# Last sum of the second pooling unit on VectorE, other PSUM pairs for the last gates, pool weights and recurrence results further forward in their queues

## The chip, the cores and the metric

One core of one Trainium2 chip runs the kernel. The metric is the device time of one execution in microseconds (us), as the median of several runs; the profile is a further execution, recorded by the hardware profiler. The engines are TensorE (PE in the profile), its weight load (PEld), VectorE (DVE), ScalarE (ACT), GpSimd (POOL) and SyncE (SP), which issues DMAs only.

## What is computed

One transformer layer in fp32, for 512 positions of 1024 channels. The reference, cut to its main line:

```python
h = rms_norm(x, norm_mix)
u_pool, u_lru, q, k, v, g_logits = split(h @ w_in)        # 1024 columns each, g_logits 3 x 1024
gates  = sigmoid(g_logits + b_gate)                       # one per branch and channel
y_pool = pool_mixer(u_pool, w_pool, pool_scale)           # means over 2, 4, 8, 16 positions, minus u;
                                                          # then a 256 x 256 product per group of channels
y_lru  = rglru_mixer(u_lru, ...)                          # gated linear recurrence along the positions
y_sb   = stick_breaking_attention(rms(q), rms(k), v)      # 8 heads of 128
merged = sum over b of gates[b] * (y[b] @ w_branch[b])
x = x + merged @ w_out
x = x + swiglu_ffn(rms_norm(x, norm_ffn))
```

## The kernel before

**Products.** Each fp32 product is made of three matmuls in a faster format. `split_w` (L135) takes a weight of 128x1024 elements apart: ScalarE writes the rounded part `whi` (L142), VectorE the rest `wlo` (L143). `product` (L354, its matmuls L359) then issues 24 matmuls of 128x256 columns. Raw weights come in by DMA from SP's queue into tiles named raw, qw (gates and q, k, v) or pw (pooling), each with few buffers: a load waits until the buffer's last reader is done.

**Seven products in place of eight.** The large projections go by a scheme of the Strassen kind: a unit of work has seven products, 11, 12, S1, S2, S3, S4 and 22, and some of them use sums of weight blocks. These sums are made in place, either by a DMA from GpSimd's queue that adds to what is in the buffer (`accum_op`), or by a VectorE addition. `add_pool7` (L255 to L269) does this for the two pooling units: `PNEXT` (L242) names for unit 1 the DMAs that accumulate (after the split of 11, S1 and S2), and unit 0 has its S4 sum on VectorE (L259). `PORDER` (L240) is the order of the products of both units.

**The order of the work around the change.** After q, k and v come the two pooling units (names u and ps_u), then four units of gates of which the last two (cc = 0 and 1, names g and ps_g) matter here. `weights` takes the next split weight from a list in fixed order (`emit_next`), up to three ahead of the product. All instructions are put into order by a scheduler that goes by the order of the code, by priorities and by which buffers are free; each engine then works through its own queue in that order, and an instruction that waits holds up all that stand behind it. Between the products `tick` and `pool_mean` (L944) issue the small operations that belong to other parts: `pool_mean` makes the moving means of the pooling branch on VectorE, and `MEAN` (L967) says behind which products.

**PSUM.** Eight banks. Through the projections they are four pairs (pool `pb`); a product unit holds one pair for X and one for Y. Two halves of a unit are read out by ScalarE early (L977, L1006), the rest is added by VectorE at the end (L982, and L938 in `gate_done` for the gates). `gate_done` then has ScalarE make the sigmoid (L940) and GpSimd's queue store the gate to memory (tiles gd, L942). After the gates the same banks are cut up anew for attention: `pmm` (3 banks, branch products ps_br), `pz` (2 banks, scores z) and `paux` (3 banks, among them the transposes pq). For the last unit the pair of ps_gy1 is banks 0 and 1 and that of ps_gx1 banks 4 and 5; the first transposes pq00 go to bank 5, the first branch product ps_br_1_0_0 to bank 0. A memset of VectorE on a tile `skip_g` takes one pair out of the rotation for this.

**What follows the gates.** For each head `trans` (L1127, matmuls L1131) transposes q and k (tiles at, loaded on SP, L1124) into pq, ScalarE and VectorE split the result (qkh L1134, qkl L1135), TensorE makes the scores z, ScalarE turns them into K and A (L1164, L1165), VectorE scans them (L1168). In between stand the products of the recurrence branch, ps_br (lines 350 to 352 within `mm3`, three matmuls of 128x512 each): their right-hand sides yHH and yHL are loaded back from memory by GpSimd's queue (L1286), their weights are raw97, raw98 and so on. `load_pool_weights` (L1072) loads the four matrices of the pooling branch (rawp, L1074, on SP) and splits them (wph L1076, wpl L1077). The merge (L450) multiplies a branch product by its gate g, which SP loads (L1101) from where `gate_done` stored it.

Of the kernel before, what the change touches and what calls it, by code (L numbers as in the profile page):

```python
# [8 lines left out]
F32 = mybir.dt.float32  # L9
# [56 lines left out]
def layer_kernel(ctx: ExitStack, tc: tile.TileContext, x, xt, vecs, w_in, w_qkv7, w_gate7, w_pool7, w_pool, w_rg, w_ig,  # L66
# [79 lines left out]
    def add_direct(key, src, a, b):  # L146
        def load(n):
            raw = wp.tile([P, a, b], F32, tag="raw", name="raw" + n)
            raws.append(nc.sync.dma_start(raw, src).ins)
            return raw  # L150

        def make(n):
            return split_w(early.pop(key, None) or load(n), [P, a, b], n)
        loads[key] = load
        specs.append((key, make))
# [86 lines left out]
    PNEXT = {"11": ("11", "21"), "S1": ("21", "11"), "S2": ("21", "12")}  # L242
# [12 lines left out]
    def add_pool7(u, nm):  # L255
        def make(n):
            if u == 0 and nm == "S4":
                r = praw[u, "12"]
                dve.tensor_tensor(r, r, praw[u, "S2"], ALU.add)  # L259
            buf = {"S1": "21", "S2": "21" if u else "S2", "S3": "11", "S4": "21" if u else "12"}.get(nm, nm)  # L260
# [222 lines left out]
    with ExitStack() as first:  # L483
# [452 lines left out]
        def gate_done(cc, j, t, ps):  # L936
            v = two2(t)
            dve.tensor_tensor(v, v, in_order2(ps), ALU.add)  # L938
            for w in range(2):
                act(t[:, w, :], t[:, w, :], AF.Sigmoid, scale=-1.0 if j else 1.0,  # L940
                    bias=vcol("b_gate", 16 + 2 * (2 * cc + w) + j))
            nc.gpsimd.dma_start(gd2[cc, j], t)  # L942
# [24 lines left out]
        MEAN = ((0, "S4"), (0, "22"), (1, "S2"), (1, "12"))  # L967
# [20 lines left out]
        for cc in range(2):  # L988
            tx, ty = (b4([2, S], f"g{n}{cc}", "bw"[cc]) for n in "xy")
            if cc:  # L990

                dve.memset(pb.tile([P, 2, S], F32, tag="mm", name="skip_g")[:, 0, 0:1], 0.0)
            Y = pb.tile([P, 2, S], F32, tag="mm", name=f"ps_gy{cc}")
            X = pb.tile([P, 2, S], F32, tag="mm", name=f"ps_gx{cc}")
# [8 lines left out]
            for nm in ORDER:  # L1003
# [9 lines left out]
                if (cc, nm) == (0, "12"):  # L1013
                    with tc.issue_after(state["acc"]):
                        q_scales()
                if cc == 0 and nm in ("S2", "S1", "S3"):
                    load_early({"S2": ("br", 1, 0, 0), "S1": ("br", 1, 0, 1), "S3": ("br", 1, 1, 0)}[nm])
                if cc and nm not in ("11", "22") and means:
# [25 lines left out]
    with ExitStack() as mix:  # L1044
# [27 lines left out]
        def load_pool_weights(g):  # L1072
            raw = rawp[g]
            nc.sync.dma_start(raw, w_pool[g].rearrange("(k p) c -> p k c", p=P))  # L1074
# [207 lines left out]
        for i in range(2):  # L1282
            yhl = [hp.tile([P, 4, S], F32R, tag=f"{t}{i}", name=f"y{t}{i}") for t in ("HH", "HL")]
            for k2 in range(2):
                for t, d in zip(yhl, yd):
                    nc.gpsimd.dma_start(t[:, 2 * k2:2 * k2 + 2, :], d[i][:, 2 * k2:2 * k2 + 2, :])  # L1286
            ylru += [tuple(t[:, k, :] for t in yhl) for k in range(4)]
        for c in range(4):
# [539 lines left out]
```

## Time and profile before

| | |
|---|---|
| median of 3 runs | 879.77 us (879.38 to 882.63) |
| the profiled execution | 886.13 us |
| its span, first to last instruction | 884.3 us |
| TensorE busy | 98% |
| VectorE, ScalarE, GpSimd busy | 85%, 60%, 11% |
| stretch of the pooling and gate units around the change | 260 to 329 us |
| start of attention and the recurrence branch | 329 to 392 us |

The profile gives busy times, not useful ones: a matmul at half clock is busy for twice as long. PEclk is the granted clock, 1.00 being full speed. In the views of instructions each row has the start, the duration, the engine, the line, the operation with its output and inputs, and in brackets how long the engine had been idle before it and what ended that. In the view of waits a row names who waited for what, with total, count and longest. In the view of stretches each row has the length, then busy time and count by engine, the granted clock, the busy share of the DMA engines, and GB/s. A DMA's row on a queue is the time of its issuing; when it has landed is told by the rows "to landing".

### The profile page before, as it was taken

The page shows a single profiled execution, that of the slowest core. Times are in us where ns is not written, and L with a number is a line of the kernel's source. Part 1 is how long each engine was busy: PE and PEld are TensorE (multiplying, and loading weights), DVE is VectorE, ACT ScalarE, POOL GpSimd, SP SyncE. Part 2 cuts the span into 40 slices and gives each one's busy share as a digit, 9 for nine tenths or more (in the row PEclk, how much of TensorE's full clock was granted, in tenths as well). Part 3 has the DMA queues.
Part 4 walks back from the last instruction along what each step waited for, and adds up shares of the span by engine and source line. Part 5 has one row for each costly group of instructions (what it writes and reads, how often), then busy time and mean ns, then how long its engine had stood idle before and what let it go on. Part 6 is the DMA issues. An engine that isn't in the chain of part 4 may idle for free.

```text
span 884.3 us, 14573 instructions
## 1 busy us (share of the span) xinstructions
PE 865.3 (98%) x5707; PEld 796.4 (90%) x5707; DVE 748.1 (85%) x949; ACT 527.8 (60%) x733; POOL 95.8 (11%) x137
## 2 busy tenths in 40 slices
PE   9999999999998997999999999999999999999998
PEld 6888878888898996888889998889999999999998
DVE  6899898989787795897989696699998988998974
ACT  6555989667853565675754544555555555754642
POOL 1110002233324111000001100000000000121200
PEclk9999999999999997999999999999999999999999
DMA  9685355998798379545645965346543434797913
GB/s 334 168 293 182 96 189 168 269 276 241 221 303 198 67 213 318 169 132 167 195 116 140 196 190 186 98 121 166 147 117 97 119 97 134 228 208 202 191 42 120
DMA packets 114469, 157.26 MB, mean 178 GB/s; under 512 B 8288, under 2 KB 86112, under 8 KB 114400
## 3 DMA queue, kind: packets, MB, share of 16 engines
q1 hardware_dynamic: 100864, 107.30, 38.2%
q0 software_dynamic: 13392, 48.76, 24.1%
q8 instruction: 45, 0.74, 0.3%
q10 hardware_dynamic: 144, 0.26, 0.1%
q14 instruction: 24, 0.20, 0.1%
HBM read 135.85 MB, written 18.87 MB: 175 GB/s over the span
## 4 chain that ended last, share of the span: by engine, by line
PE 84%; DVE 5%; ACT 5%; DMA 4%; issue 1%; SPq 0%; ACTq 0%; DVEq 0%
PE ps_y L359 11%; PE ps_q L875 8%; PE ps_x L359 8%; PE ps_dy L1746 5%; PE ps_dx L1746 4%; PE ps_br L352 3%; PE ps_br L350 3%; PE ps_br L351 3%; PE ps_bY L1370 2%; PE ps_gy L359 2%; PE ps_bX L1370 2%; PE ps_gx L359 2%; PE ps_uy L359 2%; PE ps_gate L778 2%; DVE wlo L143 1%; PE ps_lru L350 1%
## 5 line engine op out<-in xcount | busy, mean ns | idle before, releaser
L142 ACT ACTIVATE whi<-raw 128x1024 fp32r<-128x1024 f32 x58 | 61.2, 1055 | 64.6 <-PE ps_br L351 16.8
L143 DVE TENSOR_TENSOR wlo<-raw,whi 128x1024 fp32r<-128x1024 f32 x58 | 70.7, 1220 | 18.2 <-ACT whi L142 17.7
L143 DVE TENSOR_TENSOR wlo<-qw,whi 128x1024 fp32r<-128x1024 f32 x48 | 58.3, 1218 | 14.7 <-ACT whi L142 14.7
L142 ACT ACTIVATE whi<-qw 128x1024 fp32r<-128x1024 f32 x48 | 50.4, 1053 | 31.7 <-PE ps_q L875 10.4
L1531 ACT ACTIVATE wh_S<-w_S 128x1024 fp32r<-128x1024 f32 x36 | 38.2, 1061 | 28.8 <-PE ps_y L359 20.1
L1652 POOL DMA_DIRECT2D dw<-in_w_down_dram x20 | 17.4, 957 | 308.3 <-DMA dw<-in_w_down_dram 252.7
L1532 DVE TENSOR_TENSOR wl_S<-w_S,wh_S 128x1024 fp32r<-128x1024 f32 x36 | 43.8, 1218 | 3.3 <-ACT wh_S L1531 3.3
L1531 ACT ACTIVATE wh<-w 128x1024 fp32r<-128x1024 f32 x27 | 28.6, 1061 | 27.8 <-PE ps_x L359 9.4
L1532 DVE TENSOR_TENSOR wl<-w,wh 128x1024 fp32r<-128x1024 f32 x27 | 32.9, 1219 | 7.9 <-ACT wh L1531 7.9
L1531 ACT ACTIVATE whdS<-dw 128x1024 fp32r<-128x1024 f32 x20 | 21.2, 1061 | 21.6 <-PE ps_dy L1746 10.6
L1532 DVE TENSOR_TENSOR wldS<-dw,whdS 128x1024 fp32r<-128x1024 f32 x20 | 24.2, 1219 | 6.1 <-ACT whdS L1531 6.1
L351 PE MATMUL ps_br<-yHL,whi 128*128 128x512 f32 x64 | 25.6, 400 | 1.5 <-DMA yHL<-ydl 1.5
L350 PE MATMUL ps_br<-yHH,whi 128*128 128x512 f32 x64 | 25.4, 397 | 1.2 <-DVE gy L938 1.2
L1168 DVE TENSOR_TENSOR_SCAN E<-K,ahead 128x512 f32<-128x512 f32 (+3 forms) x32 | 25.3, 812 | 1.2 <-ACT K L1164 1.2
L352 PE MATMUL ps_br<-yHH,wlo 128*128 128x512 f32 x64 | 25.4, 397 | 0.0
L350 PE MATMUL ps_lru<-HH,whi 128*128 128x512 f32 x64 | 24.6, 384 | 0.0
L350 PE MATMUL ps_br<-yph,whi 128*128 128x512 f32 x64 | 24.5, 383 | 0.0
L143 DVE TENSOR_TENSOR wlo<-pw,whi 128x1024 fp32r<-128x1024 f32 x13 | 15.9, 1222 | 10.0 <-ACT whi L142 10.0
L350 PE MATMUL ps_gate<-HH,whi 128*128 128x512 f32 x64 | 24.4, 381 | 0.0
L351 PE MATMUL ps_lru<-HL,whi 128*128 128x512 f32 x64 | 24.3, 379 | 0.0
L352 PE MATMUL ps_lru<-HH,wlo 128*128 128x512 f32 x64 | 24.3, 379 | 0.0
L351 PE MATMUL ps_gate<-HL,whi 128*128 128x512 f32 x64 | 24.3, 379 | 0.0
(785 smaller groups left out, 3559.5 us busy)
## 6 DMA issues: line engine op xcount, KB each, us to landing
qw<-in_w_qkv_dram SPq DMA_DIRECT2D x24, 512.0 KB, 7.1
raw<-in_w_in_dram SPq DMA_DIRECT2D x23, 512.0 KB, 5.9
dw<-in_w_down_dram POOLq DMA_DIRECT2D x20, 512.0 KB, 7.6
w<-in_w_ffn_gate_dram SPq DMA_DIRECT2D x36, 256.0 KB, 4.0
w<-in_w_ffn_up_dram SPq DMA_DIRECT2D x36, 256.0 KB, 4.6
raw<-in_w_branch_dram SPq DMA_DIRECT2D x13, 512.0 KB, 4.0
qw<-in_w_qkv_dram POOLq DMA_DIRECT2D x12, 512.0 KB, 8.5
qd<-r POOLq DMA_DIRECT2D x12, 512.0 KB, 6.7
```

The costliest lines, as they stand in the source:

```text
L142: act(hi, raw, AF.Copy)
L143: los.append(dve.tensor_tensor(lo, raw, hi.bitcast(F32), ALU.subtract).ins)
L350: nc.tensor.matmul(ps, lh, rh, start=start, stop=False, skip_group_check=skip)
L351: nc.tensor.matmul(ps, lh, rl, start=False, stop=False, skip_group_check=skip)
L352: nc.tensor.matmul(ps, ll, rh, start=False, stop=stop, skip_group_check=skip)
L359: nc.tensor.matmul(o, a_[a][:, w, k, :], il2(b_[b][:, k, :]), start=first and n == k == 0, stop=last and n == 2 and k == 3, skip_group_che ...
L875: nc.tensor.matmul(ps[:, a, :], b_[:, k, ts_], il(a_[:, kk, :]), start=first and n == k == 0, stop=n == 2 and k == 3, skip_group_check=True)
L1168: dve.tensor_tensor_scan(E[:, c0:c0 + n][:, ::-1], K[:, c0 + 1:c0 + n + 1][:, ::-1], ahead[:, S - n:][:, ::-1], 0.0, ALU.mult, ALU.add)
L1370: nc.tensor.matmul(o, ah[x_][:, w, k, :], il2(b[k][y_]), start=first_ and n == k == 0, stop=n == 2 and k == 3, skip_group_check=True)
L1531: act(h, src, AF.Copy)
L1532: dve.tensor_tensor(l, src, h.bitcast(F32), ALU.subtract)
L1746: nc.tensor.matmul(o, a_[a][:, w, k0 + k, :], il2(b_[b][:, k, :]), start=first and i == k == 0, stop=last and i == 2 and k == nk - 1, skip ...
```

## The change

Its parts, in the order of the diff (lines behind L141 stand one to three lower in the changed kernel):

- The DMA raw97 (first of the branch weights that are not loaded early) is issued only behind the last pool weight on SP; the others follow it.
- The S4 sum of pooling unit 1 is made by VectorE, pw112 += pw121, in place of the accumulating DMA; the query scales, whose issue point hung on that DMA, now follow the accumulation behind S1.
- Three of the eight pooled means are issued in the pooling units, behind other products than the four before; one more is issued in gate unit 0, the rest in gate unit 1.
- The memset of `skip_g` is gone, and unit 1 takes its pair X first: ps_gx1 is now banks 0 and 1, ps_gy1 banks 4 and 5. A memset of GpSimd on a buffer of the raw weights (`skip_r`) is added in gate unit 0.
- On GpSimd the stores of the last two gates are put behind the loads of the recurrence results.

```diff
@@ add_direct
-            raws.append(nc.sync.dma_start(raw, src).ins)
+            with tc.issue_after(state["rawp"]) if key == ("br", 1, 1, 1) else nullcontext():
+                raws.append(nc.sync.dma_start(raw, src).ins)
@@ add_pool7
-    PNEXT = {"11": ("11", "21"), "S1": ("21", "11"), "S2": ("21", "12")}
+    PNEXT = {"11": ("11", "21"), "S1": ("21", "11")}
...
-            if u == 0 and nm == "S4":
+            if nm == "S4":
                 r = praw[u, "12"]
-                dve.tensor_tensor(r, r, praw[u, "S2"], ALU.add)
-            buf = {"S1": "21", "S2": "21" if u else "S2", "S3": "11", "S4": "21" if u else "12"}.get(nm, nm)
+                dve.tensor_tensor(r, r, praw[u, "21" if u else "S2"], ALU.add)
+            buf = {"S1": "21", "S2": "21" if u else "S2", "S3": "11", "S4": "12"}.get(nm, nm)
@@ gate_done
-            nc.gpsimd.dma_start(gd2[cc, j], t)
+            state["gd", cc, j] = nc.gpsimd.dma_start(gd2[cc, j], t).ins
@@ pooling units
-        MEAN = ((0, "S4"), (0, "22"), (1, "S2"), (1, "12"))
+        MEAN = ((1, "12"), (1, "S3"), (1, "22"))
@@ last gate units
-            if cc:
-
-                dve.memset(pb.tile([P, 2, S], F32, tag="mm", name="skip_g")[:, 0, 0:1], 0.0)
-            Y = pb.tile([P, 2, S], F32, tag="mm", name=f"ps_gy{cc}")
-            X = pb.tile([P, 2, S], F32, tag="mm", name=f"ps_gx{cc}")
+            YX = {z: pb.tile([P, 2, S], F32, tag="mm", name=f"ps_g{z}{cc}") for z in ("xy" if cc else "yx")}
+            Y, X = YX["y"], YX["x"]
...
+                if (cc, nm) == (0, "11"):
+                    nc.gpsimd.memset(wp.tile([P, 1024], F32, tag="raw", name="skip_r")[:, 0:1], 0.0)
...
-                if cc and nm not in ("11", "22") and means:
+                if (cc or nm == "S2") and nm not in ("11", "22") and means:
                     pool_mean(*means.pop(0))
@@ load_pool_weights
-            nc.sync.dma_start(raw, w_pool[g].rearrange("(k p) c -> p k c", p=P))
+            state["rawp"] = nc.sync.dma_start(raw, w_pool[g].rearrange("(k p) c -> p k c", p=P)).ins
@@ recurrence results
-                    nc.gpsimd.dma_start(t[:, 2 * k2:2 * k2 + 2, :], d[i][:, 2 * k2:2 * k2 + 2, :])
+                    load = nc.gpsimd.dma_start(t[:, 2 * k2:2 * k2 + 2, :], d[i][:, 2 * k2:2 * k2 + 2, :]).ins
             ylru += [tuple(t[:, k, :] for t in yhl) for k in range(4)]
+        for j in range(2):
+            tc.add_manual_dep(state["gd", 1, j], load.name, mybir.DependencyInfo(
+                mybir.DependencyClass.NoSync, mybir.DependencyReason.DATA), reason="order")
```

What the scheduler makes of it stands in the engines' queues. First VectorE, from wlo75 (the split for product S2 of pooling unit 1) over wlo76 (product 12) to wlo77 (S3); pw112 and pw121 are raw weight blocks of unit 1, u00 and u01 the results of unit 0, pw00 a pooled mean. The split for S4, wlo78, stands five rows behind the end of this piece. Before:

```order
L143 TENSOR_TENSOR wlo75_2498<-pw121_2171,whi75_2497 128x1024
L982 TENSOR_TENSOR u00_2272<-u00_2272,ps_ux0_2307 128x1024
L143 TENSOR_TENSOR wlo76_2533<-pw112_2213,whi76_2532 128x1024
L952 COPY pw00_2527<-u00_2272 128x1
L953 TENSOR_TENSOR pw00_2527<-u00_2272 128x511
L958 SCALAR_TENSOR_TENSOR pw00_2527<-pw00_2527,invpos_112 128x1
L982 TENSOR_TENSOR u01_2308<-u01_2308,ps_uy0_2271 128x1024
L143 TENSOR_TENSOR wlo77_2566<-pw111_2169,whi77_2565 128x1024
```

In the changed kernel, with wlo78 at the end:

```order
L143 TENSOR_TENSOR wlo75_2498<-pw121_2171,whi75_2497 128x1024
L983 TENSOR_TENSOR u00_2272<-u00_2272,ps_ux0_2307 128x1024
L143 TENSOR_TENSOR wlo76_2527<-pw112_2213,whi76_2526 128x1024
L260 TENSOR_TENSOR pw112_2213<-pw112_2213,pw121_2171 128x1024
L983 TENSOR_TENSOR u01_2308<-u01_2308,ps_uy0_2271 128x1024
L143 TENSOR_TENSOR wlo77_2556<-pw111_2169,whi77_2555 128x1024
L143 TENSOR_TENSOR wlo78_2586<-pw112_2213,whi78_2585 128x1024
```

The addition to pw112 stands ahead of the second sum u01, and the three operations of a pooled mean between wlo76 and wlo77 have gone further back, behind wlo78.

SP's queue, from the end of the gates' weights (the row after qw4220 in both) to the loads of the first gates for the merge (g100, g101). Before:

```order
L149 DMA raw97_3524<-in_w_branch_dram 128x4x256
L149 DMA raw98_3616<-in_w_branch_dram 128x4x256
L149 DMA raw99_3691<-in_w_branch_dram 128x4x256
L1074 DMA rawp0_3233<-in_w_pool_dram 128x2x256
L1074 DMA rawp1_3234<-in_w_pool_dram 128x2x256
L1074 DMA rawp2_3231<-in_w_pool_dram 128x2x256
L1074 DMA rawp3_3232<-in_w_pool_dram 128x2x256
L1124 DMA at02_3230<-qd20_88 128x4x128
L1124 DMA at10_3364<-qd00_84 128x4x128
L1124 DMA at11_3366<-qd10_86 128x4x128
L1124 DMA at12_3368<-qd20_88 128x4x128
L1101 DMA g100_3442<-gd10_94 128x512
```

In the changed kernel:

```order
L1074 DMA rawp0_3233<-in_w_pool_dram 128x2x256
L1074 DMA rawp1_3234<-in_w_pool_dram 128x2x256
L1074 DMA rawp2_3231<-in_w_pool_dram 128x2x256
L1074 DMA rawp3_3232<-in_w_pool_dram 128x2x256
L150 DMA raw97_3524<-in_w_branch_dram 128x4x256
L1124 DMA at02_3230<-qd20_88 128x4x128
L150 DMA raw98_3616<-in_w_branch_dram 128x4x256
L1124 DMA at10_3364<-qd00_84 128x4x128
L1124 DMA at11_3366<-qd10_86 128x4x128
L1124 DMA at12_3368<-qd20_88 128x4x128
L150 DMA raw99_3691<-in_w_branch_dram 128x4x256
L1101 DMA g100_3442<-gd10_94 128x512
```

The four rawp have moved ahead of raw97, and at02, at10, at11 and at12 stand between and behind the branch weights; raw99 and g100 are now behind at12. The buffer that at11 takes is one of which GpSimd's store gd211 has to be done.

GpSimd's queue, from the last load for the first two recurrence results to the store of the last gate. Before:

```order
L1286 DMA yHL0_3431<-ydl0_104 128x1024
L1286 DMA yHL1_3437<-ydl1_105 128x1024
L1286 DMA yHH1_3436<-ydh1_103 128x1024
L942 DMA gd210_100<-gx1_2959 128x1024
L1286 DMA yHH1_3436<-ydh1_103 128x1024
L942 DMA gd211_101<-gy1_2960 128x1024
L1286 DMA yHL1_3437<-ydl1_105 128x1024
```

In the changed kernel:

```order
L1286 DMA yHL0_3431<-ydl0_104 128x1024
L1286 DMA yHL1_3437<-ydl1_105 128x1024
L1286 DMA yHH1_3436<-ydh1_103 128x1024 x2
L1286 DMA yHL1_3437<-ydl1_105 128x1024
L943 DMA gd210_100<-gx1_2961 128x1024
L943 DMA gd211_101<-gy1_2962 128x1024
```

Both stores, gd210 and gd211, now stand behind all loads.

## The prediction

> **What bounds the kernel now.** I read the page first, then the view of the waits around the changed code, then the busy times of the stretches, and last the order of single instructions at each stall. The page:
>
> ```profile
> span 884.3 us, 14573 instructions
> PE 865.3 (98%) x5707; PEld 796.4 (90%) x5707; DVE 748.1 (85%) x949; ACT 527.8 (60%) x733; POOL 95.8 (11%) x137
> ```
>
> TensorE is busy for 98% of the span, so there are two ways to gain: shorten a wait of TensorE, or the time that it is busy at a lower clock. The view of what TensorE waits for between 250 and 440 us lists the first:
>
> ```profile
> PE ps_uy L359 <- ACT u L977: 2.8, 1, 2.8
> PE z L350 <- ACT A L1165: 2.3, 1, 2.3
> PE ps_br L351 <- DMA yHL<-ydl: 1.5, 1, 1.5
> PE pq L1131 <- issue: 1.5, 1, 1.5
> PE ps_br L350 <- DVE gy L938: 1.2, 1, 1.2
> PE z L351 <- DVE qkl L1135: 0.4, 1, 0.4
> ```
>
> These six rows are 9.7 us, and nearly all of them lie in the code that the change touches. The busy times of seven short stretches show the second kind of loss (columns: length, busy time and count, granted clock, share of the DMA engines, GB/s):
>
> ```profile
> 278.72:281.71 2.99, 0.17 (x3) 1.00 0.65 214
> 281.71:285.10 3.39, 3.39 (x16) 0.51 0.47 134
> 328.99:332.84 3.85, 1.24 (x11) 1.00 0.99 308
> 332.84:336.40 3.56, 3.56 (x9) 0.52 0.92 292
> 342.80:344.43 1.63, 0.15 (x1) 1.00 1.07 372
> 345.40:347.90 2.50, 0.16 (x1) 0.75 1.16 320
> 347.90:353.30 5.40, 5.40 (x14) 0.50 1.16 317
> ```
>
> After three of the four gaps TensorE runs at half clock for 3.4 to 5.4 us. That costs 3.39 x 0.49 = 1.7, 3.56 x 0.48 = 1.7 and 5.40 x 0.50 = 2.7 us, and it counts as busy. Only the gap of 1.63 us is followed by none. So there are two places to account for: stall 1 at 279 us, and stall 2, a chain of waits from 329 to 353 us.
>
> **Stall 1: the sum by VectorE (L259, L268).** ScalarE's rows and GpSimd's:
>
> ```profile
> 272.44 0.85 POOL L268 DMA_DIRECT2D pw<-in_w_pool_dram  x1 [4.03 <-DVE wlo L143]
> 280.11 1.06 ACT L142 ACTIVATE whi<-pw 128x1024 fp32r<-128x1024 f32 x1 [5.59 <-DMA pw<-in_w_pool_dram]
> 281.08 0.58 ACT L977 ACTIVATE u<-ps_uy 128x512 f32<-128x512 f32 x1
> 257.10 1.23 DVE L259 TENSOR_TENSOR pw<-pw,ps 128x1024 f32<-128x1024 f32 x1
> ```
>
> The accumulating DMA of unit 1 is issued at 272.44 and its sum is there at 280.11, when ScalarE's split of it starts. Behind that split in ScalarE's queue stands the eviction of ps_uy at 281.08, for which TensorE waits: it starts S3 at 281.71. What is late is thus not the product that needs the sum (S4, one later), but an eviction queued behind it. The change sums with a VectorE operation of the last row's shape, 1.23 us, placed behind the split wlo76. VectorE has a gap for it: in 260:282 it is busy for 12.84 of 22.00 us.
>
> ```profile
> 260.00:282.00 22.00, 19.18 (x171) 18.99 (x170) 12.84 (x16) 9.59 (x12) 10.23 (x9) 0.99 0.96 248
> 282.00:304.00 22.00, 22.00 (x185) 22.00 (x185) 19.01 (x24) 9.96 (x12) 1.83 (x2) 0.93 0.43 96
> ```
>
> The sum is then there at about 275.5, ScalarE splits it and reads ps_uy out while TensorE runs the product 12 ahead of S3, and S3 starts when TensorE is free, at 278.7. **Gain: 2.8 us of wait and 1.7 us of half clock, 4.5 us.** Lower bound 2.8, if the half clock comes after another short gap instead. What is late next: VectorE's splits of the gate weights. In 282:304 it has 3.0 us left, the new operation takes 1.2, and part of the pooled means is now issued behind these splits; so I expect no new wait here, with a slack of about 1 us. The memset that goes, the memset that GpSimd gains (in a stretch in which it has nothing due) and the later issue point of the query scales I set at nothing: none stands ahead of something that TensorE awaits.
>
> **Stall 2, first part: the other PSUM pairs.** TensorE's and VectorE's rows:
>
> ```profile
> 329.30 1.21 DVE L938 TENSOR_TENSOR gx<-gx,ps_gx 128x1024 f32<-128x1024 f32 x1
> 331.57 1.21 DVE L938 TENSOR_TENSOR gy<-gy,ps_gy 128x1024 f32<-128x1024 f32 x1
> 330.62 1.06 PE L1131 MATMUL pq<-idn,at 128*128 128x128 f32 x8 [1.46 <-issue]
> 332.84 0.69 PE L350 MATMUL ps_br<-yHH,whi 128*128 128x512 f32 x1 [1.15 <-DVE gy L938]
> ```
>
> The eight transposes pq start when VectorE has read ps_gx (329.30 + 1.21 = 330.51), the branch product when it has read ps_gy (332.78): their new PSUM tiles lie in those banks. The change swaps the pairs. Now pq lies where ps_gy was and must wait for the second sum; the branch waits for the first, but stands behind pq in TensorE's queue. So the transposes no longer fill the time between the two sums, and the branch starts 1.06 us later against the end of the gates. **Cost: 1.1 us** (bounds: 0, if VectorE reaches ps_gy sooner, to 1.1, all eight transposes). The half clock behind this gap I leave as it is.
>
> **Stall 2, second part: pool weights ahead of the branch weights (SP), recurrence results ahead of the gate stores (GpSimd).**
>
> ```profile
> 345.55 0.63 ACT L1076 ACTIVATE wph<-rawp 128x512 fp32r<-128x512 f32 x1 [4.70 <-DMA rawp<-in_w_pool_dram]
> 347.17 0.68 ACT L1165 ACTIVATE A<-z,qrs 128x512 f32<-128x512 f32 x1
> 329.41 5.13 SPq L149 DMA_DIRECT2D raw<-in_w_branch_dram  x3
> 334.60 4.36 SPq L1074 DMA_DIRECT2D rawp<-in_w_pool_dram  x4
> 339.00 7.54 SPq L1124 DMA_DIRECT2D at<-qd  x4
> rawp<-in_w_pool_dram SPq DMA_DIRECT2D x4, 256.0 KB, 10.6
> 334.50 0.54 POOL L942 DMA_DIRECT2D gd<-gy  x1 [1.19 <-ACT gy L940]
> 335.03 0.55 POOL L1286 DMA_DIRECT2D yHL<-ydl  x1
> 321.54 1.22 DVE L143 TENSOR_TENSOR wlo<-qw,whi 128x1024 fp32r<-128x1024 f32 x1
> yHL<-ydl POOLq DMA_DIRECT2D x1, 512.0 KB, 9.4
> ```
>
> The third score product z waits until ScalarE has read the first scores (A, 347.17). ScalarE stands for 4.70 us in front of the pool weight's split wph, whose load went out at 334.60, behind three branch weights that had waited in SP's queue for free buffers until 329.41. It takes 10.6 us to land. With the four loads ahead of those three, they go out when their own buffers come free; the last of these is read by VectorE's split of the gates' last but one weight (321.54 + 1.22 before, so about 318 with 4.5 us gained). Landed after 10.6 us, at 329, they are there before ScalarE arrives. **Gain: 2.3 us of wait and 2.7 us of half clock, 5.0 us**; lower bound 2.3. The last load yHL stood behind the store gd of gy (334.50) and landed 335.03 + 9.4 = 344.4, when TensorE's wait for it ends; ahead of the stores it goes out when the gates still run. **Gain: 1.5 us.** Without the pool weights the 1.5 us would only lengthen the wait for A behind it, so the two go together.
>
> **What this adds.** SP's load at11 takes the buffer of gy, which comes free when the store gd of gy has landed; behind it stand at12, a branch weight and the gates g100. The store is issued 4.5 us earlier than 334.50, at 330.0.
>
> ```profile
> gd<-gy POOLq DMA_DIRECT2D x1, 512.0 KB, 8.1
> g<-gd SPq DMA_DIRECT2D x1, 256.0 KB, 5.4
> 354.87 0.68 DVE L450 SCALAR_TENSOR_TENSOR m<-g,ps_br 128x512 f32<-128x512 f32 x1
> ```
>
> Landing after 8.1 us gives 338.1; two loads at 7.54/4 = 1.9 us and one at 5.13/3 = 1.7 us bring g100's issue to 343.6, and 5.4 us later, at 349.0, the gates are there. TensorE needs what the merge m frees (the PSUM tile of ps_br_1_1_1) 47 matmuls behind z0_2. I put z0_2 at about 341.5: 347.90, less 4.5, less the waits of 1.5 and 2.3, plus 1.1, plus 0.9 for the branch products now ahead of it. At 0.215 us apiece 47 matmuls end at 351.6, so there are 2.6 us left. In VectorE's queue the merge has two weight splits more ahead of it; and later VectorE itself is close to the bound:
>
> ```profile
> 370.00:392.00 22.00, 21.20 (x128) 18.11 (x127) 21.58 (x33) 17.33 (x36) 0.00 (x0) 1.00 0.55 162
> 392.00:530.00 138.00, 137.43 (x880) 125.85 (x879) 118.45 (x176) 80.37 (x143) 9.56 (x11) 1.00 0.62 162
> ```
>
> These two meeting points no row prices. The nearest are the waits of 0.4 (for qkl) and 1.5 us (for yHL) above; I take 0.7 for each, **cost 1.4 us**, with bounds of 0.4 and 3.0. Behind 392 us TensorE is busy for 137.43 of 138.00 us, so nothing there can take up a gain made ahead of it.
>
> **Sum.** 4.5 - 1.1 + 5.0 + 1.5 - 1.4 = 8.5 us. The profiled execution took 886.13 us (its span 884.3); it would be 877.6. The median of the runs shown is 879.77, 6.4 us under the profiled one, and I carry the difference over: 879.77 - 8.5 = **871.3 us**. Ends: all waits and half clocks gone, no cost of pq and the small cost, 4.5 + 5.0 + 1.5 - 0.4 = 10.6, and the half clock at 332.84 too, 1.7 and some tenths: 866.8 or a little under. The other way 2.8 - 1.1 + 2.3 + 1.5 - 3.0 = 2.5: 877.3. The smallest difference that a measurement here tells from none is about 0.5%, 4.4 us: faster means under 875.4.
>
> **The clock, weighed.** Gaps of 2.99 and 2.50 us are followed by half clock at 0.51 and 0.50, the one of 1.63 us is not. The Trainium skill, "TensorE: Matmul & The Clock Gate", Part 1: The HAM clock gate, says that TensorE falls to half rate after an idle window of about 3.4 us, that the windows run free of the program, and that some 3.4 us of work bring it back. By that threshold neither gap had to throttle, and the 4.4 us of clock in my gains would be chance; the trace disagrees with it on the gap's length and agrees roughly on the return (3.39 us, but also 5.40).
>
> **Rivals.**
> *Only stall 1 pays.* VectorE, 21.58 of 22.00 us in 370:392, becomes the bound and stall 2's gain is given back there: 4.5 - 0.7 = 3.8, 876.0. For it: that row. Against it: from 329 to 347 VectorE idles for half of the time, waiting for the same loads, and would start earlier too. Chance 0.10.
> *The half clock stays.* It depends on where a window falls, not on a gap's length, and each stretch comes back after some gap that remains (the one at the gates' end does): 8.5 - 1.7 - 2.7 = 4.1, 875.7. For it: the 1.63 us gap without one. Against it: three of three gaps of 2.5 us and more have one. Chance 0.07.
> *VectorE's queue is too full at stall 1.* The sum delays a split of the gates, and TensorE waits there: with 4.5 lost, 4.0 is left, 875.8. Speaks for it: 19.01 of 22.00 us; against it: the 3.0 us left. Chance 0.05.
> *Slower: SP stands behind the store.* at11 holds up g100 and all later loads. From a landing of the store 2.6 us beyond 338.1 on, each us is one of TensorE's. With 9 us of wait and two half clock stretches behind it (1.7 + 2.7), 13.4 us, it outweighs the gain: 884.7. That needs store and load together to take 25 us instead of 13.5; the slowest landing in the rows above is 10.6. Chance 0.07.
> *The change doesn't reach the wait.* z's wait is set by something that came at the same time as rawp, and S3's by another eviction: about 879.8. Against it: the two releasers are named in ScalarE's rows with 5.59 and 4.70 us of idling. Chance 0.03.
>
> **Chances.** The forecast, with all terms within their bounds, has 0.68. Faster by over 0.5%: the forecast and a little of the three rivals at 876, 0.70. Within 0.5%: the rest of these and the last, 0.23. Slower: 0.07. The range from 866.5 to 877.3 leaves out the slower rival, the last one and some tails of the forecast, near 0.2.
>
> **What would show it.** The profile after should have no wait of ps_uy for u, with S3 at full clock; the transposes pq waiting for gy's sum, near 328; wph with no wait for rawp; no wait for yHL; half clock once, not twice, between 329 and 353; and a small wait, if any, of ps_br for the merge. A long row of SP ahead of at11 with a wait of TensorE for m would prove me wrong, as would VectorE busy all through 282:304 with TensorE waiting for wlo.

## The result, and the profile after

The changed kernel takes 876.12 us (median of 8 runs, 874.58 to 878.29); before took 880.25 us (8 runs, 879.38 to 882.94) on the same chip: a ratio of 0.9948, 95% interval 0.9931 to 0.9965. It is 4.1 us faster (3.1 to 6.1 by the interval), where 8.5 were forecast; 876.12 lies inside the forecast's range, near its upper end. A second comparison on another chip, below, gave 875.54 against 881.13 us, 0.9927 (0.9903 to 0.9951). Ratios and intervals throughout come from the comparison with the kernel before on the same chip, and need not be the quotient of the two medians. One execution of fill (3193.81 us) and one of best_no_sum (1107.16 us) stood far outside all others and are left out of their medians below.

The profiled executions lie much further apart than the medians: 874.58 us after, 886.13 us before. The page after:

```profile
span 872.8 us, 14573 instructions
PE 859.7 (98%) x5707; PEld 791.0 (91%) x5707; DVE 748.5 (86%) x949; ACT 528.3 (61%) x733; POOL 96.6 (11%) x137
```

What TensorE waits for between 250 and 440 us, in full:

```profile
PE pq L1131 <- issue: 3.7, 1, 3.7
PE pq L1131 <- DVE wtl L1184: 0.4, 1, 0.4
PE ps_uy L360 <- DVE wlo L143: 0.3, 1, 0.3
PE pps L352 <- DVE p00l L1041: 0.3, 1, 0.3
PE pw L1181 <- DVE qkl L1135: 0.3, 1, 0.3
PE py L351 <- DVE wtl L1184: 0.2, 1, 0.2
```

The waits for u, for A and for yHL are gone. One has grown: pq waits 3.7 us where it waited 1.5. Single instructions, stall 1 first:

```profile
276.07 1.23 DVE L260 TENSOR_TENSOR pw<-pw,pw 128x1024 f32<-128x1024 f32 x1
277.41 1.07 ACT L142 ACTIVATE whi<-pw 128x1024 fp32r<-128x1024 f32 x1 [2.52 <-DVE pw L260]
278.39 0.57 ACT L978 ACTIVATE u<-ps_uy 128x512 f32<-128x512 f32 x1
279.06 0.32 PE L360 MATMUL ps_uy<-hT3h,whi 128*128 128x256 f32 x1
```

The sum takes 1.23 us, ScalarE's split follows it, the eviction follows the split, and S3 starts at 279.06 with no gap (281.71 before). There is little to spare: the eviction ends 0.1 us before S3 starts (278.39 + 0.57 = 278.96), as the sum is there at 277.30, where I had put 275.5. Stall 2:

```profile
325.53 1.22 DVE L939 TENSOR_TENSOR gx<-gx,ps_gx 128x1024 f32<-128x1024 f32 x1
327.80 1.22 DVE L939 TENSOR_TENSOR gy<-gy,ps_gy 128x1024 f32<-128x1024 f32 x1
329.11 1.94 PE L1131 MATMUL pq<-idn,at 128*128 128x128 f32 x8 [3.72 <-issue]
331.68 0.62 ACT L1076 ACTIVATE wph<-rawp 128x512 fp32r<-128x512 f32 x1
300.28 19.11 SPq L1074 DMA_DIRECT2D rawp<-in_w_pool_dram  x4
324.45 0.57 POOL L1286 DMA_DIRECT2D yHL<-ydl  x1
339.14 0.98 SPq L1101 DMA_DIRECT2D g<-gd  x2
```

The transposes start when gy's sum is done (327.80 + 1.22 = 329.02). The pool weights go out between 300 and 320 us and ScalarE's split wph no longer waits. The last yHL goes out at 324.45. The gates for the merge are issued at 339.14, 4.5 us earlier than I had put them (343.6), and no wait for the merge appears.

The clock, in stretches of 3.41 us (length, TensorE's busy time and count, granted clock, DMA share, GB/s):

```profile
325.02:328.44 3.42, 0.37 (x4) 1.00 0.93 244
328.44:331.85 3.41, 2.74 (x11) 0.50 1.06 361
331.85:335.26 3.41, 3.41 (x18) 1.00 1.07 384
```

One half clock stretch is left between 250 and 800 us, behind the grown gap.

**Where the time went, by parts of the program.** All kernels make their weight splits in the same order on VectorE, so the same split marks the same place in each. Two of the marks as VectorE's rows show them, first in the kernel before:

```profile
328.17 1.22 DVE L143 TENSOR_TENSOR wlo<-rawbr,whi 128x1024 fp32r<-128x1024 f32 x1
...
421.76 1.23 DVE L143 TENSOR_TENSOR wlo<-raw,whi 128x1024 fp32r<-128x1024 f32 x1 [0.18 <-ACT whi L142]
```

The same two in the changed kernel:

```profile
324.40 1.22 DVE L143 TENSOR_TENSOR wlo<-rawbr,whi 128x1024 fp32r<-128x1024 f32 x1
...
413.98 1.23 DVE L143 TENSOR_TENSOR wlo<-raw,whi 128x1024 fp32r<-128x1024 f32 x1 [0.19 <-ACT whi L142]
```

From the first to the second it is 93.59 us before and 89.58 after: the attention start gains 4.0. In the same way the pooling and gate units (from the split at 254.10 us before, 253.86 after, to the first mark) go from 74.06 to 70.54, 3.5 less, and a part of the FFN near 800 us (from the split at 771.28 to the one at 821.32 us before) from 50.05 to 46.17, 3.9 less. These three make up 11.4 of the 11.5 us between the spans. Nothing of the change touches the FFN.

### The profile page after: what moved, and what is told of

It reads as the page before. It is cut to its first block, busy times and chain, and to the rows that moved or that the text cites. A ratio compares the mean times of both kernels' runs of the same rounds, so it can differ in the third digit from the quotient of the medians.

```text
span 872.8 us, 14573 instructions
## 1 busy us (share of the span) xinstructions
PE 859.7 (98%) x5707; PEld 791.0 (91%) x5707; DVE 748.5 (86%) x949; ACT 528.3 (61%) x733; POOL 96.6 (11%) x137
## 4 chain that ended last, share of the span: by engine, by line
PE 87%; DVE 5%; ACT 4%; issue 2%; DMA 1%; SPq 0%; DVEq 0%; ACTq 0%
PE ps_y L360 11%; PE ps_q L876 8%; PE ps_x L360 8%; PE ps_dy L1749 6%; PE ps_dx L1749 5%; PE ps_br L351 3%; PE ps_br L352 3%; PE ps_br L353 3%; PE ps_bY L1373 2%; PE ps_gy L360 2%; PE ps_gate L779 2%; PE ps_gx L360 2%; PE ps_uy L360 2%; PE ps_bX L1373 2%; PE ps_lru L351 1%
## 5 line engine op out<-in xcount | busy, mean ns | idle before, releaser
L143 DVE TENSOR_TENSOR wlo<-raw,whi 128x1024 fp32r<-128x1024 f32 x58 | 70.9, 1223 | 12.3 <-ACT whi L142 11.4
L1534 ACT ACTIVATE whdS<-dw 128x1024 fp32r<-128x1024 f32 x20 | 21.3, 1063 | 21.0 <-PE ps_dy L1749 10.6
```

What stands on the lines that cost most here:

```text
L143: los.append(dve.tensor_tensor(lo, raw, hi.bitcast(F32), ALU.subtract).ins)
L1534: act(h, src, AF.Copy)
```

## The experiments

Kernel names: S is the sum on VectorE, R the pool weights first on SP, Y the recurrence results first on GpSimd, P the swapped PSUM pairs. Kernels derived from the changed one also keep its other small moves (the pooled means, the memset of GpSimd), which no run takes apart; sum_only without them and old_pairs with them differ by 0.2 us in the first column. The table puts all 14 profiles side by side, in the three parts just named, with the half clock windows of 3.41 us in each up to the FFN (+1: one more in the FFN part). The column "windows per run" is an estimate over all timed executions: what the mean granted clock on record lacks to 1.00, times the span, divided by 1.7 us, the time that one such window takes away. It counts half clock anywhere in the kernel, and as each clock is recorded to 0.001 it is good to about half a window. The last three rows move one mean across the mark between the first two columns, so only their sum compares with the others.

| kernel | has | pooling and gates | attention start | FFN part | half clock | windows per run | median (before, same chip) |
|---|---|---|---|---|---|---|---|
| before | - | 74.06 | 93.59 | 50.05 | 4+1 | 3.4 | 880.25 |
| pair_only | P | 71.96 | 92.84 | 47.98 | 1 | 2.7 | 881.12 (881.13) |
| sum_only | S | 69.55 | 94.18 | 49.88 | 3+1 | 3.2 | 880.72 (881.14) |
| yh_only | Y | 70.60 | 89.38 | 47.16 | 0 | 1.1 | 876.76 (881.31) |
| rawp_only | R | 74.57 | 89.98 | 46.18 | 2 | 1.4 | 875.92 (881.31) |
| rawp_yh | R Y | 71.64 | 87.40 | 50.08 | 0+1 | 0.9 | 876.54 (881.14) |
| no_sum | R Y P | 72.20 | 89.88 | 46.44 | 1 | 1.5 | 877.47 (881.14) |
| after | S R Y P | 70.54 | 89.58 | 46.17 | 1 | 1.7 | 876.12 (880.25) |
| after_again | S R Y P | 69.33 | 89.94 | 48.14 | 1 | 1.1 | 875.54 (881.13) |
| old_pairs | S R Y | 69.35 | 87.40 | 48.31 | 0 | 0.9 | 873.79 (881.14) |
| fill | S R Y P | 69.35 | 87.61 | 46.19 | 0 | 0.2 | 871.94 (881.13) |
| pairs_gy_late | S R Y | 68.51 | 87.62 | 48.90 | 0 | 0.1 | 869.75 (881.13) |
| best_again | S R Y | 67.17 | 87.63 | 46.18 | 0 | 0.3 | 871.72 (881.31) |
| best_no_sum | R Y | 70.97 | 87.56 | 46.18 | 1 | 0.5 | 873.52 (881.31) |

The new column says what the profiles alone can't. An execution of the kernel before has 3.4 such windows in the mean (65 executions on three chips), not the 5 of the one that was profiled, and the kernels with R or Y or both have 0.1 to 1.7. From one execution to the next of the same kernel on one chip, a window more goes with about 1.6 us more, by a straight line through all 175. So about 3 to 4 of the 4.1 to 5.6 us that the change gains in the median go with half clock that is gone; this is an estimate, as half clock and the waits that bring it come together.

The theories at the start: (1) the forecast's, that each term is worth in the median what it cost in the profile of before; (2) that the profiled execution of before was worse than the usual one at the very places that the change mends, so that the medians move less. From the clock records of the first profiles came (3): half clock goes by a fixed grid of windows.

**sum_only.** The kernel before with only the sum changed:

```diff
-    PNEXT = {"11": ("11", "21"), "S1": ("21", "11"), "S2": ("21", "12")}
+    PNEXT = {"11": ("11", "21"), "S1": ("21", "11")}
...
-            if u == 0 and nm == "S4":
+            if nm == "S4":
...
```

> The kernel before with the S4 sum of pooling unit 1 on VectorE alone. If the profile of before shows a usual execution, S3 of unit 1 no longer waits for the eviction (2.8 us) and no half clock follows (1.7 us): 4.5 us less than before. If the profiled execution of before (886.13 us, 6 us above the median) shows longer waits and more half clock than the usual one, the landing it waits for is earlier as a rule: 1 to 2.5 us less. If the sum only fills VectorE's queue: no difference, with new waits of TensorE for wlo between 280 and 300 us.

Measured: 0.999 (0.9968 to 1.0012), so 0.4 us less in the median, between 2.8 less and 1.1 more. Its profile has no wait of S3, and its pooling and gates take 69.55 us, the shortest so far. But behind the gates it is no faster than before. TensorE's three longest waits between 250 and 440 us:

```profile
PE ps_br L351 <- DMA yHL<-ydl: 2.9, 1, 2.9
PE pq L1131 <- issue: 1.4, 1, 1.4
PE z L350 <- ACT A L1165: 1.4, 1, 1.4
```

And the row of ScalarE's split of the first pool weight:

```profile
340.79 0.63 ACT L1076 ACTIVATE wph<-rawp 128x512 fp32r<-128x512 f32 x1 [6.66 <-DMA rawp<-in_w_pool_dram]
```

The wait for yHL has grown from 1.5 to 2.9, ScalarE's for the pool weights from 4.7 to 6.7, and three half clock windows lie here, as before. TensorE ran at full clock up to there and stood longer for the same landings. Nor do the timed executions lose half clock by the sum: 3.2 windows each, against 3.4 before. Theory 1 falls for this term.

**rawp_yh.** The kernel before with R and Y alone:

```diff
+            with tc.issue_after(state["rawp"]) if key == ("br", 1, 1, 1) else nullcontext():
...
+            tc.add_manual_dep(state["gd", 1, j], load.name, mybir.DependencyInfo(
+                mybir.DependencyClass.NoSync, mybir.DependencyReason.DATA), reason="order")
```

> The kernel before with the two moves in the queues alone: pool weights ahead of the branch weights on SP, recurrence results ahead of the gate stores on GpSimd. By the forecast's terms the waits of 1.5 and 2.3 us and one half clock stretch of 2.7 us go, less 1.4 us of new waits: 5 us less than before. If the usual execution has shorter waits there than the profiled one: 1 to 3 us less. If SP stands behind the gate store: a wait of TensorE for the merge, and no gain or a loss.

Measured: 0.9944 (0.9924 to 0.9963), 4.6 us less in the median: the forecast's 5 holds, and these two moves carry most of what the whole change brings. The attention start takes 87.40 us, 6.2 less, without any half clock.

**old_pairs.** The changed kernel with the pairs of before:

```diff
-            YX = {z: pb.tile([P, 2, S], F32, tag="mm", name=f"ps_g{z}{cc}") for z in ("xy" if cc else "yx")}
-            Y, X = YX["y"], YX["x"]
+            if cc:
+                dve.memset(pb.tile([P, 2, S], F32, tag="mm", name="skip_g")[:, 0, 0:1], 0.0)
+            Y = pb.tile([P, 2, S], F32, tag="mm", name=f"ps_gy{cc}")
+            X = pb.tile([P, 2, S], F32, tag="mm", name=f"ps_gx{cc}")
```

> The changed kernel with the PSUM pairs of before (ps_gy1 first, and the memset that skips a pair). By the forecast the transposes fill the time between the two sums again: the first branch product 1.1 us earlier against the end of the gates, 1.1 us less than the changed kernel. If a half clock stretch follows the gap in both and takes up the difference, or the DMAs behind the store of gy set what follows: the same time as the changed kernel within 0.5 us.

Measured: 873.79 us, 0.9928 (0.9901 to 0.9955) of before. The changed kernel ran on two other chips, with 876.12 us (0.9948) and 875.54 us (0.9927); the intervals overlap, so the medians alone don't show what the pairs cost. The profiles do: the attention start takes 87.40 us here, against 89.58, 89.94 and 89.88 in the three profiles with R, Y, P and an empty gap. By these the swap costs 2.2 to 2.5 us, twice the forecast's 1.1. A half clock window (1.7 us) is the greater part: all four profiles with P and an empty gap have it, pair_only among them, and this one has not.

**no_sum.** The changed kernel with the accumulating DMA:

```diff
-    PNEXT = {"11": ("11", "21"), "S1": ("21", "11")}
+    PNEXT = {"11": ("11", "21"), "S1": ("21", "11"), "S2": ("21", "12")}
...
-            if nm == "S4":
+            if u == 0 and nm == "S4":
...
```

> The changed kernel with the accumulating DMA for the S4 sum of unit 1, as before. If the parts add up and the forecast's size of 4.5 us holds: 4.5 us more than the changed kernel. If the usual gain of the sum is half of that: 1 to 2.5 us more. If the parts are not additive because the time won at the sum is lost again at the gates' end: the same as the changed kernel.

Measured: 0.9963 (0.9944 to 0.9982), 877.47 us. The changed kernel had 0.9948 and 0.9927 on two other chips, so the DMA costs 1.3 to 3.2 us by these, with intervals that overlap. S3 waits for the eviction again, but no half clock follows:

```profile
PE ps_uy L360 <- ACT u L978: 2.6, 1, 2.6
```

So the usual cost of this stall looks nearer 2 than 4.5 us.

**after_again, fill, pairs_gy_late, pair_only** ran on one chip. The first is the changed kernel once more, with no edit:

> The changed kernel once more, as the yardstick for the three others on this chip. By the clock records of six profiles TensorE runs at half clock for a window of 3.413 us after a window of a fixed grid in which it was busy for less than about half. In the gap of 3.7 us at the gates' end nearly every position of the grid has such a window, so: one half clock stretch behind that gap, as in the first profile, and some 4 us less than before. If half clock there was chance: none in about half of the profiles.

Measured: 875.54 us, 0.9927 (0.9903 to 0.9951). The gap of 3.72 us and one half clock window are there again.

**fill** adds, behind the last product of the gates:

```diff
+        wps = pb.tile([P, 2, S], F32, tag="mm", name="fill_ps")
+        for i in range(14):
+            nc.tensor.matmul(wps[:, 0, :], warm, warm.unsqueeze(1).to_broadcast([P, 4, P]), start=True, stop=True)
```

> The changed kernel with 14 extra matmuls of constants (about 3 us) into an unused PSUM pair, put into TensorE's queue behind the last gate product, so that the gap of 3.7 us is filled; nothing of the result is changed. If half clock follows from a window with too little work: none behind this gap, and 1 to 1.7 us less than the changed kernel, though the branch product starts no earlier. If it is set by something else than TensorE's own work (the waits, the DMA): the same time as the changed kernel.

Measured: 871.94 us, 0.9889 (0.9864 to 0.9915), 3.6 us less than after_again, by work that nobody needs; each of these five executions was faster than each of after_again. The stretches around its gap (length, TensorE's busy time and count, clock, DMA share, GB/s):

```profile
324.20:328.00 3.80, 3.15 (x15) 1.00 0.89 239
328.00:331.50 3.50, 3.47 (x20) 1.00 1.07 372
331.50:335.00 3.50, 3.50 (x18) 1.00 1.07 399
```

The half clock is gone, and with it 2.3 us of the attention start (87.61 against 89.94). That is more than the 1.7 us of a window; where the other 0.6 come from the rows don't say, as the eight transposes take 1.06 us in both. That half clock follows from too little work of TensorE, and that it was most of what the swap cost, is thereby shown: the transposes and the branch product start as late here as in after_again, and yet this attention start is only 0.2 us longer than that of old_pairs. The remaining 1.3 of the median's 3.6 us lie elsewhere (the FFN part differs by 1.9 in the two profiles).

**pairs_gy_late** is old_pairs with two more moves: the last pooled mean behind the gates, and the last sum of the gates ahead of the split wlo95.

```diff
+            state["lo" + n] = los[-1]
...
+            add = dve.tensor_tensor(v, v, in_order2(ps), ALU.add).ins
+            if cc and j:
+                tc.add_manual_dep(state["lo95"], add.name, mybir.DependencyInfo(
+                    mybir.DependencyClass.NoSync, mybir.DependencyReason.DATA), reason="order")
...
+        pool_mean(*means.pop(0))
```

> The changed kernel with the PSUM pairs of before, the last pooled mean issued behind the gates and the last sum of the gates ahead of the split wlo95 on VectorE. The sum of gx can start when S4's product is done, that of gy when 22's is; from the rows of the changed kernel (wlo93 at 321.08, two operations of 1.13 us to the end of gx, gy's sum from 325.5 to 326.7) the branch product starts at about 326.7 in place of 330.2: 3.4 us less wait than the changed kernel, and no half clock (1.7 us): 5 us less than the changed kernel, 2 to 2.5 less than with the old pairs alone. If the next thing behind the gap (gates stored, at11, g100) sets the pace: 1 us less or nothing against the old pairs.

Measured: 869.75 us, 0.9866 (0.9839 to 0.9892), 5.8 less than after_again, as expected (5). VectorE's rows for the two sums:

```profile
323.47 1.22 DVE L940 TENSOR_TENSOR gx<-gx,ps_gx 128x1024 f32<-128x1024 f32 x1
325.62 1.22 DVE L940 TENSOR_TENSOR gy<-gy,ps_gy 128x1024 f32<-128x1024 f32 x1 [0.93 <-PE ps_gy L361]
```

TensorE's rows for what waits for them:

```profile
325.35 1.04 PE L1139 MATMUL pq<-idn,at 128*128 128x128 f32 x8
326.90 0.48 PE L352 MATMUL ps_br<-yHH,whi 128*128 128x512 f32 x1 [0.51 <-DVE gy L940]
```

VectorE now waits for TensorE, not the other way; of 3.7 us of waiting 0.5 are left.

**pair_only.** The kernel before with the swap alone:

```diff
-                dve.memset(pb.tile([P, 2, S], F32, tag="mm", name="skip_g")[:, 0, 0:1], 0.0)
...
+            YX = {z: pb.tile([P, 2, S], F32, tag="mm", name=f"ps_g{z}{cc}") for z in ("xy" if cc else "yx")}
...
```

> The kernel before with the swapped PSUM pairs alone. By the forecast the first branch product starts 1.1 us later: 1.1 us more than before. With the grid of clock windows the gap without any matmul grows to 3.7 us and a half clock stretch is nearly certain, where before it came in a part of the executions: 1.5 to 2.5 us more. If the waits for yHL and the pool weights behind it take the delay up, since their landing doesn't move: no difference.

Measured: 881.12 against 881.13 us, 0.9999 (0.9979 to 1.0018): no difference, within 1.9 us less and 1.6 more. TensorE's longest waits behind the gates:

```profile
PE pq L1131 <- issue: 3.7, 1, 3.7
PE z L350 <- ACT A L1162: 2.3, 1, 2.3
PE ps_br L351 <- DMA yHL<-ydl: 1.3, 1, 1.3
```

The same gap of 3.7 us and the same half clock as in the changed kernel, yet no price is measured. That TensorE then waits for yHL and the pool weights in any case, so that the swap has a price only where those waits have been taken away, is an argument. This profile does not show it: the two waits are hardly shorter than before (1.5 and 2.3 us there), and the two half clock windows behind them are missing, with 1.49 us of work in the window ahead (shown at the end) where it was 1.13 before. Nor do the timed executions have more half clock than before: 2.7 windows against 3.4.

**rawp_only, yh_only, best_again, best_no_sum** were compared on one further chip. R and Y apart, each on the kernel before; rawp_only:

```diff
+            with tc.issue_after(state["rawp"]) if key == ("br", 1, 1, 1) else nullcontext():
...
```

> The kernel before with the pool weights ahead of the branch weights on SP alone. If the landing of the pool weights sets the end of the stretch behind the gates, as the wait of 2.3 us and the half clock behind it say, this alone brings most of the 4.6 us of both moves: 3 to 5 us less than before, with the wait for yHL (1.3 to 2.9 us) left. If yHL sets it: 0 to 1 us less.

Measured: 0.9934 (0.9912 to 0.9956), 5.4 us less in the median, a little more than expected; the wait for yHL is 2.3 us, as expected.

yh_only:

```diff
+        for j in range(2):
+            tc.add_manual_dep(state["gd", 1, j], load.name, mybir.DependencyInfo(
...
```

> The kernel before with the loads of the recurrence results ahead of the gate stores alone. The wait for yHL (1.5 us) goes, but TensorE then waits as much longer for the pool weights: no difference from before (the forecast said so). If the two waits are independent: 1.5 us less.

Measured: 0.9953 (0.9933 to 0.9972), 4.5 us less, where I expected none. The loads of SP have the same order as before, but ScalarE's wait for the first pool weight is shorter (4.70 before):

```profile
339.55 0.63 ACT L1076 ACTIVATE wph<-rawp 128x512 fp32r<-128x512 f32 x1 [2.62 <-DMA rawp<-in_w_pool_dram]
```

The median time from issue to landing of the four loads, where it was 10.6 (10.8 in sum_only, 10.7 in pair_only):

```profile
rawp<-in_w_pool_dram SPq DMA_DIRECT2D x4, 256.0 KB, 8.8
```

In the kernel before, two loads of the recurrence results are issued at 332.77 and 335.03, beside the pool weights at 334.60; here they are out of the way, and the pool weights land 1.8 us sooner. That the one follows from the other is argued from these rows, not tried by itself. And a wait of TensorE for a result of ScalarE, p00h, takes 1.5 us, in place of the 1.5 and 2.3 us for yHL and A:

```profile
PE pps L350 <- ACT p00h L1040: 1.5, 1, 1.5
```

So R and Y are largely two ways to the same gain; together they bring, in the medians, no more than one alone (4.6 us on one chip, 5.4 and 4.5 on the other). The profiles have the attention start 2 to 2.6 us shorter with both (87.40 against 89.38 and 89.98), and the intervals are too wide to rule that out.

best_again is pairs_gy_late with no further edit:

> The fastest version so far (old pairs, last mean behind the gates, last gate sum ahead of wlo95) once more: 869.75 on the chip of the last comparison, 11 us less than before; the same is expected here, 10.5 to 12 us less.

Measured: 871.72 us, 0.989 (0.9864 to 0.9915): 9.6 us less, a little under the expectation. By the first of its two comparisons (0.9866) it is the fastest version here; by this one it is level with fill (0.9889).

best_no_sum is the same with the accumulating DMA:

```diff
-            if nm == "S4":
+            if u == 0 and nm == "S4":
...
```

> The same version with the accumulating DMA for the S4 sum of unit 1. By the profiles so far the stretch from the pooling units to the gates' end takes 71.6 to 72.2 us with the DMA (74.1 where a half clock window follows the wait) and 69.4 us with VectorE's sum, and nothing behind it can take this up any more: 2.3 us more than the version with the sum, 3 to 4 if half clock follows the wait in most executions. By the forecast's 4.5 us: 4.5 more. If the median of the sum alone (0.4 us) is what it is worth: under 1 us more.

Measured: 873.52 us, 0.9909 (0.9882 to 0.9936), 1.8 more than best_again; single executions of the two overlap (871.4 to 874.4 against 869.06 to 872.99). The two profiles differ by 3.7 us in the sum of the first two columns (158.53 against 154.80), with a wait of 1.9 us and a half clock window behind it:

```profile
278.19:281.60 3.41, 1.51 (x13) 1.00 0.56 214
281.60:285.01 3.41, 3.41 (x18) 0.50 0.48 155
```

So the sum on VectorE is worth about 2 us in the median here, with an uncertainty of about that size. That it is worth more than in sum_only because nothing behind it takes the gain up fits these runs, but is not shown.

## Why the prediction was right in its way and too large in size

**Stall 1 (4.5 us forecast).** The mechanism was right: S3 waits no more, and ScalarE's queue shows why. The size was not. In the seven profiles with the accumulating DMA the wait is 0.98 to 3.34 us (2.82 in the one that I read), and half clock follows in three of the seven (before, rawp_only, best_no_sum). By the first column the six profiles with the DMA and the same marks average 72.5 us, the five with the sum 69.6: 2.9 us, and in the medians 1.3 to 3.2 (no_sum, across chips) and 1.8 (best_no_sum). The profiled execution had both a long wait and the half clock. On its own the sum shows 0.4 us, with an interval to 2.8; the half clock of the whole kernel stays with it (3.2 windows per execution against 3.4). How much of the gain the waits behind the gates then swallow as a rule, one profile can't say, and it stays open.

**The PSUM pairs (-1.1 us forecast).** The step that failed is "the half clock behind this gap I leave as it is". It was there in the profile of before, but with the old pairs the gap (1.46 and 1.15 us with transposes between) is followed by half clock in one profile of six (before; not sum_only, rawp_yh, old_pairs, rawp_only, yh_only). With the swapped pairs it is one gap of 3.72 us, and half clock follows in four of four. The term is -2.2 to -2.5 us by the profiles. The later start, for which I had set 1.1, is the smaller part of it: fill has it without the half clock, and loses 0.2 against old_pairs.

**Pool weights and recurrence results (5.0 + 1.5 us).** Both waits went, and 6.2 us of the attention start with them in rawp_yh; its median shows 4.6 us. That this is near 6.5 less the 1.4 of new waits confirms nothing, as those waits were set too large. "The two go together" and "the 1.5 us would only lengthen the wait for A" were wrong: Y alone brought 4.5 us, and the landing of the pool weights, which I had reckoned as fixed at 10.6 us, came down to 8.8 with it.

**New waits (-1.4 us).** Too large. The wait for the merge did not come; the gates were issued at 339.14. What is new are waits of 0.3 and 0.4 us for p00l and wtl, and one of 0.3 us in S3 for its split wlo, where I had expected none. VectorE's load is heavier than I thought (21.53 of 22.00 us busy from 282 to 304, by the profile after) without a wait of TensorE there:

```profile
282.00:304.00 22.00, 22.00 (x198) 21.90 (x197) 21.53 (x29) 11.07 (x14) 1.95 (x4) 1.00 0.50 121
```

**The sum.** Against the profiled execution it is close: 3.5 + 4.0 = 7.5 us in the two places where 8.5 were forecast, and 4.0 against 5.0 + 1.5 - 1.1 - 1.4 = 4.0 at the second. That last agreement is luck: the swap cost over 1 us more than I had set, and the two moves with their new waits brought as much more (6.2 us in rawp_yh against 5.0 + 1.5 - 1.4 = 5.1). The failure is the last step, "I carry the difference over". It took for granted that the 6.4 us by which the profiled execution exceeded the median lay somewhere else. A part lay in stall 1 (74.06 us where the other five of those six average 72.2), and by the granted clocks the profiled execution had 1.6 half clock windows, 2.7 us, more than the mean of its kernel. Another part lay in the FFN:

```profile
804.41 1.06 ACT L1531 ACTIVATE whd<-dr 128x1024 fp32r<-128x1024 f32 x1 [6.83 <-DMA dr<-in_w_down_dram]
```

A load that lands late there, and in three of the 14 profiles a half clock window behind it, make that part 46.2 to 50.1 us long, whatever the kernel. What makes the load late was not tried.

**The rivals.** *The half clock stays* was nearest, with its 875.7 us too: 1.1 to 1.7 windows per execution are left in the changed kernel. Against it I held that three of three gaps had one, and in the other profiles gaps of 1.80, 2.34 and 2.60 us had none. *Only stall 1 pays* is the reverse of what happened. *VectorE's queue* came with 0.3 us only, *SP behind the store* not at all, nor *The change doesn't reach the wait*: both waits went.

## What to carry to other kernels

One profiled execution that is slower than the median has extra waits and half clock somewhere, and a gain worked out from it is in danger of counting them: take a second profile, or compare its parts with a related kernel's, before a wait is turned into a saving. Two gaps with a little work between them can be cheaper than one gap of the same sum, as the clock falls for a window that is nearly empty. And the price of a gap can depend on what waits behind it: the swapped pairs cost nothing that could be measured on the kernel before, and 2.2 us or more by the profiles of the changed one. Where a profile is not enough, the granted clock of all timed executions tells whether half clock was lost or won.

## What the runs showed of the hardware

Half clock comes in whole windows of 3.413 us on a grid that pays no regard to the program. In the profile of before the clock's records (start in us, length in windows) are:

```
281.77 1.0    332.97 1.0    346.63 2.0    807.42 1.0
```

The starts are 15.0, 19.0 and 154.0 windows behind the first. What decides is how long TensorE was busy in the window ahead. Three windows of the kernel before, each with the one behind it:

```profile
278.36:281.77 3.41, 0.59 (x6) 1.00 0.68 233
281.77:285.18 3.41, 3.41 (x16) 0.50 0.49 144
329.56:332.97 3.41, 1.20 (x9) 1.00 0.99 309
332.97:336.38 3.41, 3.41 (x9) 0.50 0.93 294
343.21:346.63 3.42, 1.13 (x4) 1.00 1.09 361
346.63:350.04 3.41, 2.14 (x7) 0.50 1.21 299
```

A window with 1.66 us in old_pairs, not followed by half clock:

```profile
323.90:327.32 3.42, 1.66 (x14) 1.00 0.92 223
327.32:330.73 3.41, 2.56 (x12) 1.00 1.02 345
```

One with 1.49 us in pair_only, not followed by half clock either:

```profile
344.69:348.10 3.41, 1.49 (x8) 1.00 1.17 298
348.10:351.52 3.42, 3.10 (x13) 1.00 1.01 304
```

From 200 us to the end of the 14 profiles, windows at full clock with up to 1.3 us of work were followed by half clock every time, those with 2.0 us or more never; between 1.5 and 1.9 us both occur (1.51 in best_no_sum fell). Thus a gap of 2.82 us may or may not cost 1.7 us more, by where the grid lies, while one of 3.72 nearly empties a window in most positions: of the 26 timed executions of the kernels with R, Y, P and an empty gap, one shows a granted clock of 1.000. The Trainium skill, "TensorE: Matmul & The Clock Gate", Part 1, has the window of 3413 ns and that it runs free; the trace agrees with both. It asks for an idle window, and here one that is a third full was enough.
